# Sixteen gate products, four pool products and eight sums of squares: from fp32 matmuls to products of high and low parts

## The chip, the cores and the metric

The kernel runs on one core of a Trainium2 chip. Its time is the device time of one execution, in microseconds (us). A median is that of several executions; a profile is one further execution, recorded by the hardware profiler. The engines are TensorE (PE, with its weight loads as PEld), VectorE (DVE), ScalarE (ACT), GpSimd (POOL) and SyncE (SP), which here only issues DMAs.

## The reference

Two layers work on x of 512 tokens by 1024 channels, all in float32. A layer is a half-step SwiGLU feed-forward network (FFN), a token mixer, and a second FFN; an RMSNorm ends the whole. The mixer projects its normed input once (`proj = h @ w_in`) and splits the result among three branches. The three places that matter here are these:

```
# branch A, pooling: centred window means minus the token, then a map per group of 64 channels
mixed = einsum('bsgc,gcd->bsgd', mixed, pool_w)
# branch B, differential attention: RMSNorm of each head's output
o = o * rsqrt(mean(o * o, axis=-1) + SUBLN_EPS) * subln_g
# branch C, RG-LRU, in two directions: xf is a depthwise conv of lx over the tokens, width 4
r = sigmoid(einsum('bsgc,gcd->bsgd', xb, w_a) + b_a)
i = sigmoid(einsum('bsgc,gcd->bsgd', xb, w_x) + b_x)
a = exp(-8 * r * softplus(-lam)); u = sqrt(-expm1(2 * log a)) * (i * xf); h = scan(a, u)
```

Each branch is projected to 1024 channels, gated, summed, and projected once more.

## The kernel before

All activations stand channel by channel on the 128 partitions, with the 512 tokens along the free axis, so nearly every product is a 128x128 weight tile times a 128x512 tile. The large products are done in fp32r, a float32 form that PE takes in one pass and that holds fewer bits. To keep the accuracy each operand is split in two: `hilo(src)` copies the source into an fp32r tile on ACT (the high part) and puts a subtraction for DVE (source minus high: the low part) on the list `later`. `flush()` records what is on that list. `mm3` is then three matmuls into one PSUM bank: high by high, weight high by data low, weight low by data high. Weights are split in the same way, into `wh` (ACT) and `wl` (DVE). A few small products are left as plain fp32 matmuls: the LRU gates `r` and `i` (weights `bd`, data `xf`), the pool map (`bdp` by `pw`), and the attention's sums of squares `nrm` (a matrix of ones by `q`, the square of a head's output `o`).

All the instructions of an engine run in the order in which they are recorded, and the order is that of a list `units`. A unit is a stretch of PE work, mostly 24 matmuls on one weight block. After each unit comes a `gap`: here the list `later` is flushed, hooks run (`add_hook(n, fn)` puts `fn` into the gap of unit n), weights of later units are split, and side threads get a turn. The side threads are lists of steps: "lru" (conv, gates, scans), "pool" (window means, pool map), "sc" and "av" (scores and weighted values of the attention). A step runs in a gap if it lies at least as many gaps behind the step before it as its entry says (`apart`), and if a rough clock that the program keeps for ACT and DVE is not too far ahead of the one that it keeps for PE. That clock counts an fp32 matmul four times, so the change alters it a little.

The mixer begins with the two units of `lx` (named `ps<-z,wh` and `ps<-z,wl` in the trace). Ahead of them x is transposed (`zt`) and split into eight pairs of `z`; the first four are made in one gap, by four ACT instructions for the high parts and four DVE instructions for the low parts. Then `mixer_R` makes R, the norm factor of each token, and `lx` is scaled by it. The units of `v` follow, and between them run the steps of "lru": a conv for each of the two channel tiles (one ACT and three DVE instructions on a tile of `xf`), then four pairs of gates, one `r` and one `i` matmul each, and ACT and DVE work on them. Later come the units of q and k, gate logits and, at the end of the mixer, the units `y`, which project the branches; the last of them (`y<-at`) multiply the normed attention output `at`, which waits for `nrm` of the last head.

In the trace nearly every instruction has line L83, that of the helper that records them, so that they are told apart by the names of their tiles.

Of the kernel before, what the change touches and what calls it, by code (L numbers as in the profile page):

```python
# [107 lines left out]
def trunk_kernel(ctx, tc, xn, pm, fin, cst, bd, f1i, f1o, win, wbp, wba, wbl, wout, f2i, f2o, out):  # L108
# [29 lines left out]
    def f(t):  # L138
        return t.bitcast(F32)
# [8 lines left out]
    def hilo(src, name):  # L148

        hi, lo = pair(F32R, name)  # L150
        A.activation(out=hi, in_=src, func=AF.Copy)
        later.append(lambda: V.tensor_tensor(out=lo, in0=src, in1=f(hi), op=SUB))
        return hi, lo

    def mm3(acc, wh, wl, zh, zl, first, last):
        PE.matmul(acc, lhsT=wh, rhs=zh, start=first, stop=False)
        PE.matmul(acc, lhsT=wh, rhs=zl, start=False, stop=False)
        PE.matmul(acc, lhsT=wl, rhs=zh, start=False, stop=last)
# [5 lines left out]
    sp4 = cp_.tile([128, DEPTH * 4], F32, tag="sp4", name="sp4")  # L164
    nlam = cp_.tile([128, DEPTH], F32, tag="nlam", name="nlam")
    subg = cp_.tile([128, DEPTH], F32, tag="subg", name="subg")
    ident = cs[:, C_ID:C_ID + 128]
    ones = cs[:, C_ONE:C_ONE + 128]

# [16 lines left out]
    def add_hook(i, fn):  # L186
        hooks.setdefault(i, []).append(fn)
# [9 lines left out]
        V.scalar_tensor_tensor(out=r, in0=t, scalar=1.5, in1=y0, op0=ADD, op1=MUL)  # L197
        return r

    def inv_rms_start(acc, n, eps, col):  # L200

        ps = bank("nrm")
        PE.matmul(ps, lhsT=ones, rhs=acc, start=True, stop=True)
        y0, m = two("y0")
        A.t += 2.6
        A.activation(out=y0, in_=ps, func=AF.Abs_reciprocal_sqrt, scale=1.0 / n, bias=cs[:, C_EPS + col:C_EPS + col + 1])
        V.tensor_scalar(out=m, in0=ps, scalar1=1.0 / n, scalar2=eps, op0=MUL, op1=ADD)
        return y0, m
# [499 lines left out]
    def mixer(l, side, done, between):  # L708
# [20 lines left out]
        def conv(c):  # L729
            if c == 0:  # L730
                xf[:] = two("xf")
            t = xf[c]
            A.activation(out=t, in_=lx[c], func=AF.Identity, scale=pc(l, "cw", 2 * 2 + c), bias=pc(l, "cb", c))
            for j, (o0, o1, i0) in ((0, (2, S, 0)), (1, (1, S, 0)), (3, (0, S - 1, 1))):
                V.scalar_tensor_tensor(
                    out=t[:, o0:o1], in0=lx[c][:, i0:i0 + o1 - o0], scalar=pc(l, "cw", 2 * j + c), in1=t[:, o0:o1], op0=MUL, op1=ADD)
            lx[c] = None

        def lru_gate(d, c):
            e = d * 2 + c  # L740
            r, i = bank("r"), bank("i")
            PE.matmul(r, lhsT=g["bd"][:, e * 128:(e + 1) * 128], rhs=xf[c], start=True, stop=True)
            PE.matmul(i, lhsT=g["bd"][:, (4 + e) * 128:(5 + e) * 128], rhs=xf[c], start=True, stop=True)
            (th, ix), (a, t) = two("thr"), two("a")
            A.activation(out=th, in_=r, func=AF.Tanh, scale=0.5, bias=hab[:, l * 8 + e:l * 8 + e + 1])
            A.activation(out=ix, in_=i, func=AF.Tanh, scale=0.5, bias=hab[:, l * 8 + 4 + e:l * 8 + 5 + e])
            sc = sp4[:, l * 4 + e:l * 4 + e + 1]
            A.activation(out=a, in_=th, func=AF.Exp, scale=sc, bias=sc)
            A.activation(out=t, in_=th, func=AF.Tanh, scale=sc, bias=sc)
            A.activation(out=th, in_=a, func=AF.Square)  # L750
            lru[d, c] = (a, t, ix, th)
# [99 lines left out]
        def pool_win(c):  # L851
            P = pads.pop(c)
            W, o = big(name="padw"), slot(name="pw")
            tt = lambda out_, i0, i1: V.tensor_tensor(out=out_, in0=i0, in1=i1, op=ADD)
            if c == 0:
                tt(o[0:64], P[0:64, 15:527], P[0:64, 16:528])
                tt(W[64:128, 0:543], P[64:128, 0:543], P[64:128, 1:544])
                tt(o[64:128], W[64:128, 14:526], W[64:128, 16:528])
            else:
                tt(W[:, 0:543], P[:, 0:543], P[:, 1:544])  # L860
                tt(W[:, 0:541], W[:, 0:541], W[:, 2:543])
                tt(o[0:64], W[0:64, 12:524], W[0:64, 16:528])
                tt(W[64:128, 0:537], W[64:128, 0:537], W[64:128, 4:541])
                tt(o[64:128], W[64:128, 8:520], W[64:128, 16:528])
            e0 = C_EDGE + c * 16
            for t0, k in ((0, 0), (S - 8, 8)):
                V.tensor_tensor(out=o[:, t0:t0 + 8], in0=o[:, t0:t0 + 8], in1=cs[:, e0 + k:e0 + k + 8], op=MUL)
            V.scalar_tensor_tensor(out=o, in0=o, scalar=cs[:, C_INVW + c:C_INVW + c + 1], in1=P[:, 16:528], op0=MUL, op1=SUB)
            g["pw", c] = o

        def pool_mm(c):
            ps = bank("pool")
            PE.matmul(ps, lhsT=g["bdp"][:, c * 128:(c + 1) * 128], rhs=g.pop(("pw", c)), start=True, stop=True)
            hi, lo = pair(F32R, "ph")
            A.activation(out=hi, in_=ps, func=AF.Copy, scale=pc(l, "ps", c))
            V.scalar_tensor_tensor(out=lo, in0=ps, scalar=pc(l, "ps", c), in1=f(hi), op0=MUL, op1=SUB)
            g["pool", c] = (hi, lo)
# [148 lines left out]
        def subln_sq(h):  # L1026
            o, q = two("o")
            V.tensor_copy(out=o, in_=av.pop(h))
            A.activation(out=q, in_=o, func=AF.Square)
            g["o", h] = (o, q)  # L1030

        def subln(h):
            o, q = g.pop(("o", h))
# [99 lines left out]
        def load_bd():  # L1133
            g["bd"], g["bdp"] = big(name="bd"), slot(name="bdp")[:, 0:256]
            SP.dma_start(out=g["bd"], in_=bd[l][:, 0:1024])
            SP.dma_start(out=g["bdp"], in_=bd[l][:, 1024:1280])


        n0 = len(units)
        b = proj(OFF_LX)  # L1140
        for c in range(2):
            tile128(b, c, after_lx(c))
        add_hook(n0, load_bd)
        v_units()

        def qkheads(h0):
# [202 lines left out]

    def derived_steps():  # L1350
        def halves():
            for l in range(DEPTH):
                V.tensor_scalar(out=hmb[:, l * 24:l * 24 + 24], in0=pcs(l, "mb"), scalar1=0.5, scalar2=None, op0=MUL)
                V.tensor_scalar(out=hab[:, l * 8:l * 8 + 8], in0=pcs(l, "bab"), scalar1=0.5, scalar2=None, op0=MUL)
                V.tensor_scalar(out=subg[:, l:l + 1], in0=pcs(l, "sub"), scalar1=1.0 - LAM_INIT[l], scalar2=None, op0=MUL)


        n = DEPTH * 4
        lam = par[:, LAM0:LAM0 + n]
        w, q, s, p = small(n), small(n), small(n), small(n)  # L1360

        def start():
            A.activation(out=w, in_=lam, func=AF.Abs)
            A.activation(out=w, in_=w, func=AF.Exp, scale=-1.0)
            V.tensor_scalar(out=q, in0=w, scalar1=2.0, scalar2=None, op0=ADD)
            V.reciprocal(q, q)
            V.tensor_tensor(out=s, in0=w, in1=q, op=MUL)
            V.tensor_tensor(out=q, in0=s, in1=s, op=MUL)
            V.memset(p, 0.0)

        def series(ns):
            for k in ns:
                V.scalar_tensor_tensor(out=p, in0=p, scalar=1.0 / k, in1=q, op0=ADD, op1=MUL)

        def end():
            V.scalar_tensor_tensor(out=p, in0=p, scalar=1.0, in1=s, op0=ADD, op1=MUL)
            V.tensor_scalar(out=w, in0=lam, scalar1=-1.0, scalar2=0.0, op0=MUL, op1=MAX)
            V.scalar_tensor_tensor(out=w, in0=p, scalar=2.0, in1=w, op0=MUL, op1=ADD)
            V.tensor_scalar(out=sp4, in0=w, scalar1=-4.0, scalar2=None, op0=MUL)


        pr = small(2 * DEPTH)

        def lam_dot():
            for l in range(DEPTH):
                lp = pcs(l, "lp")
                V.tensor_tensor(out=pr[:, 2 * l:2 * l + 1], in0=lp[:, 0:1], in1=lp[:, 1:2], op=MUL)
                V.tensor_tensor(out=pr[:, 2 * l + 1:2 * l + 2], in0=lp[:, 2:3], in1=lp[:, 3:4], op=MUL)

        def lam_sum():  # L1390
            ps = bank("lam")
            PE.matmul(ps[:, 0:2 * DEPTH], lhsT=ones, rhs=pr, start=True, stop=True)
            e = small(2 * DEPTH)
            A.activation(out=e, in_=ps[:, 0:2 * DEPTH], func=AF.Exp)
            for l in range(DEPTH):
                V.tensor_tensor(out=nlam[:, l:l + 1], in0=e[:, 2 * l + 1:2 * l + 2], in1=e[:, 2 * l:2 * l + 1], op=SUB)
                V.tensor_scalar(out=nlam[:, l:l + 1], in0=nlam[:, l:l + 1], scalar1=-LAM_INIT[l], scalar2=None, op0=ADD)

        yield 0.5, halves, True
        yield 0.8, start, True  # L1400
        yield 0.8, lambda: series((19, 17, 15, 13, 11)), True
        yield 0.8, lambda: series((9, 7, 5, 3)), True
        yield 0.8, end, True
        yield 0.4, lam_dot, True
        yield 0.4, lam_sum, True
# [214 lines left out]
```

## Time and profile before

| what | value |
|---|---|
| median of 3 runs | 2115.81 us (2114.51 to 2118.64) |
| the profiled execution | 2117.74 us, of which its span is 2115.9 us |
| PE busy | 2072.8 us, 98% of the span |
| DVE busy | 1658.6 us, 78% |
| ACT busy | 1191.2 us, 56% |
| mean granted clock of TensorE | 0.997 of full speed |

PE is busy nearly all the time, so that the span is the sum of its matmuls and of some waits: it exceeds PE's busy time by 43.1 us. The busy time of a matmul counts from its start to its end, and matmuls overlap: what a matmul adds to the span is the distance from its start to that of the next, not its length.

### The profile page before, as it was taken

The numbers are of one execution on the slowest core, as the hardware profiler recorded it, in microseconds if no ns is written. First come the engines' busy times: TensorE is split into PE (matmuls) and PEld (weight loads), VectorE is DVE, ScalarE is ACT, GpSimd is POOL, SyncE is SP. The second block draws the span as 40 slices with busy tenths as digits, with TensorE's granted clock in tenths as the row PEclk, the third lists the DMA queues.
The fourth block names the chain that finished last, engine by engine and source line by source line (L and its number), as shares of the span: only waits on it lengthen the run. The fifth ranks groups of instructions, "written<-read, shape, count | busy, mean of one in ns | idle before, by whom it ended". The sixth has DMA issues, their size and how long they took to land.

```text
span 2115.9 us, 26228 instructions
## 1 busy us (share of the span) xinstructions
PE 2072.8 (98%) x9646; PEld 1734.1 (82%) x9646; DVE 1658.6 (78%) x2362; ACT 1191.2 (56%) x1766; POOL 343.7 (16%) x292
## 2 busy tenths in 40 slices
PE   8999999999999999999999999999999999999998
PEld 6988888788787889888879887887887877988786
DVE  6788898597677588779977878986967766788797
ACT  7555566645663565556755555665456536555564
POOL 1312230000000022213213222300000001322230
PEclk9999999999999999999999999999999999999999
DMA  9987997022226379889959879940221364887994
GB/s 252 180 184 159 210 193 216 1 79 90 70 80 189 80 148 193 162 203 196 228 104 205 172 157 239 183 154 20 84 82 54 117 180 79 163 192 164 205 179 102
DMA packets 194096, 314.61 MB, mean 149 GB/s; under 512 B 10544, under 2 KB 86832, under 8 KB 193968
## 3 DMA queue, kind: packets, MB, share of 16 engines
q0 software_dynamic: 76288, 138.43, 39.5%
q1 hardware_dynamic: 117392, 174.30, 24.8%
q8 instruction: 75, 1.23, 0.2%
q14 instruction: 53, 0.43, 0.1%
q10 hardware_dynamic: 288, 0.21, 0.0%
HBM read 310.80 MB, written 2.10 MB: 148 GB/s over the span
## 4 chain that ended last, share of the span: by engine, by line
PE 80%; DVE 9%; ACT 4%; DMA 4%; issue 2%; POOL 1%; DVEq 0%; SPq 0%; POOLq 0%; ACTq 0%
PE P L83 26%; PE Q L83 19%; PE ps L83 18%; PE o L83 4%; PE y L83 4%; DVE wl L83 4%; DMA raw<-in_f1i_dram 2%; PE v L83 2%; PE ht L83 2%; PE sc L83 1%; PE av L83 1%; ACT wh L83 1%; ACT zh L83 1%; DVE c L83 1%; DVE x L83 1%
## 5 line engine op out<-in xcount | busy, mean ns | idle before, releaser
L83 DVE TENSOR_TENSOR wl<-raw,wh 128x1024 fp32r<-128x1024 f32 (+2 forms) x696 | 705.7, 1038 | 163.4 <-ACT wh L83 153.7
L83 ACT ACTIVATE wh<-raw 128x1024 fp32r<-128x1024 f32 (+2 forms) x695 | 606.9, 906 | 208.2 <-DMA raw<-in_f2i_dram 53.0
L83 PE MATMUL ps<-z,wh 128*128 128x512 f32 x1216 | 380.1, 393 | 0.2
L372 POOL DMA_DIRECT2D raw<-in_f2i_dram x96 | 116.0, 1240 | 1114.4 <-DVE mg L83 353.2
L83 PE MATMUL P<-wl,zh 128*128 128x512 f32 (+1 forms) x768 | 287.3, 374 | 7.2 <-DVE wl L83 7.1
L83 PE MATMUL P<-wh,zh 128*128 128x512 f32 (+1 forms) x768 | 288.7, 376 | 4.7 <-ACT wh L83 3.1
L83 PE MATMUL P<-wh,zl 128*128 128x512 f32 (+1 forms) x768 | 286.5, 373 | 0.5 <-DVE zl L83 0.5
L83 PEld LDWEIGHTS ps<-z,wh 128*128 128x128 f32 x1216 | 227.1, 188 | 51.1 <-issue 3.4
L83 PE MATMUL ps<-z,wl 128*128 128x512 f32 x608 | 237.0, 390 | 0.0
L83 PE MATMUL Q<-wl,zh 128*128 128x512 f32 (+1 forms) x576 | 214.6, 373 | 6.1 <-DVE wl L83 6.1
L83 PE MATMUL Q<-wh,zh 128*128 128x512 f32 (+1 forms) x576 | 216.7, 376 | 2.1 <-ACT zh L83 1.9
L83 PE MATMUL Q<-wh,zl 128*128 128x512 f32 (+1 forms) x576 | 214.2, 372 | 1.0 <-DVE zl L83 1.0
L372 POOL DMA_DIRECT2D raw<-in_f1i_dram x96 | 116.1, 1236 | 366.9 <-DVE wl L83 274.2
L83 PEld LDWEIGHTS P<-wl,zh 128*128 128x128 f32 x768 | 145.1, 189 | 30.5 <-DVE wl L83 10.4
L83 PEld LDWEIGHTS P<-wh,zh 128*128 128x128 f32 x768 | 144.8, 189 | 25.7 <-ACT wh L83 3.5
L83 PEld LDWEIGHTS P<-wh,zl 128*128 128x128 f32 x768 | 145.0, 189 | 21.3 <-DVE zl L83 1.0
L83 PE MATMUL P<-wl,ah 128*128 128x512 f32 x352 | 138.1, 392 | 2.4 <-DVE wl L83 2.3
L83 PE MATMUL P<-wh,ah 128*128 128x512 f32 x352 | 137.5, 391 | 0.0
L83 PE MATMUL P<-wh,al 128*128 128x512 f32 x352 | 137.2, 390 | 0.0
L83 PEld LDWEIGHTS ps<-z,wl 128*128 128x128 f32 x608 | 114.1, 188 | 23.7
L83 PEld LDWEIGHTS Q<-wl,zh 128*128 128x128 f32 x576 | 108.2, 188 | 23.1 <-DVE wl L83 9.2
L83 PEld LDWEIGHTS Q<-wh,zh 128*128 128x128 f32 x576 | 108.2, 188 | 17.3 <-ACT zh L83 2.7
(192 smaller groups left out, 3414.4 us busy)
## 6 DMA issues: line engine op xcount, KB each, us to landing
raw<-in_win_dram SPq DMA_DIRECT2D x84, 512.0 KB, 4.7
raw<-in_f1i_dram POOLq DMA_DIRECT2D x64, 512.0 KB, 6.9
raw<-in_f2i_dram POOLq DMA_DIRECT2D x64, 512.0 KB, 6.9
raw<-in_f2i_dram SPq DMA_DIRECT2D x52, 512.0 KB, 5.5
raw<-in_f1i_dram SPq DMA_DIRECT2D x50, 512.0 KB, 6.2
raw<-in_f1o_dram POOLq DMA_DIRECT2D x40, 512.0 KB, 7.9
raw<-in_f2o_dram POOLq DMA_DIRECT2D x40, 512.0 KB, 8.3
raw<-in_f1o_dram SPq DMA_DIRECT2D x30, 512.0 KB, 7.5
```

What stands on the lines that cost most here:

```text
L83: return fn(*args, **kw)
L372: return lambda raw: GP.dma_start(out=raw[:, 0:n * w].rearrange("p (k f) -> p k f", f=w), in_=src, accum_op=ADD)
```

## The change

The three kinds of fp32 products become fp32r products of split parts. A gate (`lru_gate`) and a pool map (`pool_mm`) are now `mm3`, three matmuls; a sum of squares is two, a matrix of ones (`oner`, copied once at the start) by the high and by the low part of `q`. So each operand has to be split: `xf` into `xs` at the end of its conv, the pooled tile into `pw`, the squares into `qs`, and the gate and pool weights into `bh`, `bl` and a pair `bdp`, in a new function `split_bd`. That runs as a hook in the gap ahead of the first `lx` unit, and the hook that loads those weights is moved eight gaps earlier. A low part that `hilo` puts on the list is recorded at the next flush.

```diff
+    oner = cp_.tile([128, 128], F32R, tag="oner", name="oner")
...
-    def inv_rms_start(acc, n, eps, col):
+    def inv_rms_start(parts, n, eps, col):
         ps = bank("nrm")
-        PE.matmul(ps, lhsT=ones, rhs=acc, start=True, stop=True)
+        for i, part in enumerate(parts):
+            PE.matmul(ps, lhsT=oner, rhs=part, start=i == 0, stop=i == 1)
...
             lx[c] = None
+            g["xf", c] = hilo(t, "xs")
...
-            PE.matmul(r, lhsT=g["bd"][:, e * 128:(e + 1) * 128], rhs=xf[c], start=True, stop=True)
-            PE.matmul(i, lhsT=g["bd"][:, (4 + e) * 128:(5 + e) * 128], rhs=xf[c], start=True, stop=True)
+            bh, bl = g["bd"]
+            for ps, o in ((r, e * 128), (i, (4 + e) * 128)):
+                mm3(ps, bh[:, o:o + 128], bl[:, o:o + 128], *g["xf", c], True, True)
...
-            g["pw", c] = o
+            g["pw", c] = hilo(o, "pw")
...
-            PE.matmul(ps, lhsT=g["bdp"][:, c * 128:(c + 1) * 128], rhs=g.pop(("pw", c)), start=True, stop=True)
+            bh, bl = (a[:, c * 128:(c + 1) * 128] for a in g["bdp"])
+            mm3(ps, bh, bl, *g.pop(("pw", c)), True, True)
...
-            g["o", h] = (o, q)
+            g["o", h] = (o, hilo(q, "qs"))
...
+        def split_bd():
+            both = pair(F32R, "bdp")
+            for name, (hi, lo) in (("bd", (big(F32R, "bh"), big(F32R, "bl"))), ("bdp", [a[:, 0:256] for a in both])):
+                src = g[name]
+                A.activation(out=hi, in_=src, func=AF.Copy)
+                later.append(lambda lo=lo, src=src, hi=hi: V.tensor_tensor(out=lo, in0=src, in1=f(hi), op=SUB))
+                g[name] = (hi, lo)
...
-        add_hook(n0, load_bd)
+        add_hook(n0 - 8, load_bd)
+        add_hook(n0 - 1, split_bd)
```

Where the instructions go is shown at two places of the first layer's mixer; the second layer has the same rows. First ACT, from the norm of x (`m`) at the mixer's start to the table load ahead of the first gate's tanh. Before:

```order
186 L83 ACTIVATE m<-m 128x2
187 L83 ACTIVATE wh<-raw 128x512 x2
188 L83 ACTIVATE z<-zt,par 128x512 x4
189 L83 ACTIVATE R<-rb 128x512
190 L83 ACTIVATE wh<-raw 128x512 x2
191 L83 ACTIVATE xf<-lx,par 128x512 x2
192 L83 ACT_TABLE_LOAD
```

And of the change:

```order
186 L83 ACTIVATE m<-m 128x2
187 L83 ACTIVATE bh<-bd 128x1024
188 L83 ACTIVATE bdp<-bdp 128x256
189 L83 ACTIVATE wh<-raw 128x512 x2
190 L83 ACTIVATE z<-zt,par 128x512 x4
191 L83 ACTIVATE R<-rb 128x512
192 L83 ACTIVATE wh<-raw 128x512 x2
193 L83 ACTIVATE xf<-lx,par 128x512
194 L83 ACTIVATE xs<-xf 128x512
195 L83 ACTIVATE xf<-lx,par 128x512
196 L83 ACTIVATE xs<-xf 128x512
197 L83 ACT_TABLE_LOAD
```

The high parts `bh` and `bdp` stand ahead of the two weight splits and the high parts of `z`, and the high part `xs` of each conv stands between that conv and the next. On DVE, at the mixer's start, before:

```order
322 L83 TENSOR_SCALAR m<-m 128x2
323 L83 TENSOR_TENSOR m<-m 128x2
324 L83 TENSOR_TENSOR wl<-raw,wh 128x512 x2
325 L83 SCALAR_TENSOR_TENSOR z<-zt,par,z 128x512 x4
326 L83 TENSOR_SCALAR rb<-cst,m 128x128 x4
```

And of the change:

```order
323 L83 TENSOR_SCALAR m<-m 128x2
324 L83 TENSOR_TENSOR m<-m 128x2
325 L83 TENSOR_TENSOR bl<-bd,bh 128x1024
326 L83 TENSOR_TENSOR bdp<-bdp 128x256
327 L83 TENSOR_TENSOR wl<-raw,wh 128x512 x2
328 L83 SCALAR_TENSOR_TENSOR z<-zt,par,z 128x512 x4
329 L83 TENSOR_SCALAR rb<-cst,m 128x128 x4
```

The low parts `bl` and `bdp` now stand ahead of the weights' low parts and the four of `z`. Further on DVE, from `lx` to the work on the first gate, where the rows of 510 and 511 tokens are the conv steps, three for each tile. Before:

```order
327 L83 TENSOR_TENSOR lx<-ps,R 128x512 x2
328 L83 SCALAR_TENSOR_TENSOR xf<-lx,par,xf 128x510
329 L83 SCALAR_TENSOR_TENSOR xf<-lx,par,xf 128x511 x2
330 L83 SCALAR_TENSOR_TENSOR xf<-lx,par,xf 128x510
331 L83 SCALAR_TENSOR_TENSOR xf<-lx,par,xf 128x511 x2
332 L83 TENSOR_TENSOR wl<-raw,wh 128x512 x2
```

And of the change:

```order
330 L83 TENSOR_TENSOR lx<-ps,R 128x512 x2
331 L83 SCALAR_TENSOR_TENSOR xf<-lx,par,xf 128x510
332 L83 SCALAR_TENSOR_TENSOR xf<-lx,par,xf 128x511 x2
333 L83 SCALAR_TENSOR_TENSOR xf<-lx,par,xf 128x510
334 L83 SCALAR_TENSOR_TENSOR xf<-lx,par,xf 128x511 x2
335 L83 TENSOR_TENSOR xs<-xf,xs 128x512 x2
336 L83 TENSOR_TENSOR wl<-raw,wh 128x512 x2
```

Both low parts of `xf` stand behind the six conv steps, in one row. PE's own order there, before:

```order
1541 L83 MATMUL v<-wh,z 128x512
1542 L83 MATMUL r<-xf,bd 128x512
1543 L83 MATMUL i<-xf,bd 128x512
1544 L83 MATMUL v<-wh,z 128x512
1545 L83 MATMUL v<-wl,z 128x512
```

And of the change:

```order
1541 L83 MATMUL v<-wh,z 128x512
1542 L83 MATMUL r<-xs,bh 128x512 x2
1543 L83 MATMUL r<-xs,bl 128x512
1544 L83 MATMUL i<-xs,bh 128x512 x2
1545 L83 MATMUL i<-xs,bl 128x512
1546 L83 MATMUL v<-wh,z 128x512
1547 L83 MATMUL v<-wl,z 128x512
```

The gate still stands at the same place among the matmuls of `v`; its second matmul is the first to read a low part.

## Rows read from the trace of the kernel before

**Rows 1.** The page: busy time by engine; chain that ended last, by engine.
```profile
...
PE 2072.8 (98%) x9646; PEld 1734.1 (82%) x9646; DVE 1658.6 (78%) x2362; ACT 1191.2 (56%) x1766; POOL 343.7 (16%) x292
...
PE 80%; DVE 9%; ACT 4%; DMA 4%; issue 2%; POOL 1%; DVEq 0%; SPq 0%; POOLq 0%; ACTq 0%
```

**Rows 2.** Windows: us, busy us (count) by engine, PEclk, DMA share, GB/s.
```profile
...
340.00:700.00 360.00, 358.13 (x1596) 290.70 (x1595) 266.83 (x471) 192.49 (x328) 2.41 (x2) 1.00 0.30 92
1385.00:1745.00 360.00, 358.12 (x1596) 290.67 (x1595) 266.96 (x471) 192.51 (x328) 2.41 (x2) 1.00 0.30 92
1080.70:1083.70 3.00, 3.00 (x8) 2.34 (x7) 1.91 (x2) 1.06 (x2) 1.20 (x1) 0.50 0.04 6
```

**Rows 3.** Timeline of PE, first gate: start, us, engine, instruction, count.
```profile
...
376.61 1.02 PE L83 MATMUL r<-xf,bd 128*128 128x512 f32 x2
377.47 1.02 PE L83 MATMUL i<-xf,bd 128*128 128x512 f32 x2
```

**Rows 4.** Timeline of PE around one matmul of squares.
```profile
...
533.08 0.39 PE L83 MATMUL ps<-z,wl 128*128 128x512 f32 x1
533.31 1.02 PE L83 MATMUL nrm<-o,cst 128*128 128x512 f32 x2
...
534.63 0.40 PE L83 MATMUL ps<-z,wl 128*128 128x512 f32 x1
```

**Rows 5.** Timeline of ACT and DVE ahead of the first gate.
```profile
...
371.83 1.14 ACT L83 ACTIVATE wh<-raw 128x512 fp32r<-128x512 f32 x2
...
372.87 1.51 ACT L83 ACTIVATE xf<-lx,par 128x512 f32<-128x512 f32 x2
...
373.71 4.55 DVE L83 SCALAR_TENSOR_TENSOR xf<-lx,par,xf 128x510 f32<-128x510 f32 x6 [0.45 <-ACT xf L83]
...
378.18 1.28 DVE L83 TENSOR_TENSOR wl<-raw,wh 128x512 fp32r<-128x512 f32 x2
```

**Rows 6.** Timeline, start of the first layer's mixer: PE, ACT and DVE.
```profile
...
362.27 1.14 ACT L83 ACTIVATE wh<-raw 128x512 fp32r<-128x512 f32 x2
...
363.09 1.91 PE L83 MATMUL zt<-cst,x 128*128 128x128 f32 x16
363.13 1.29 DVE L83 TENSOR_TENSOR wl<-raw,wh 128x512 fp32r<-128x512 f32 x2
363.79 2.43 ACT L83 ACTIVATE z<-zt,par 128x512 fp32r<-128x512 f32 x4 [0.38 <-PE zt L83]
364.51 2.73 DVE L83 SCALAR_TENSOR_TENSOR z<-zt,par,z 128x512 fp32r<-128x512 f32 x4
...
364.75 1.06 PE L83 MATMUL ps<-z,wh 128*128 128x512 f32 x2
```

**Rows 7.** Groups by form: busy time, mean ns; idle before, its end.
```profile
...
L83 ACT ACTIVATE wh<-raw 128x1024 fp32r<-128x1024 f32 x403 | 413.7, 1052 | 141.8 <-DMA raw<-in_f2i_dram 53.0 <-DMA raw<-in_f1i_dram 48.8 <-DVE wl L83 24.6
...
L83 DVE TENSOR_TENSOR wl<-raw,wh 128x1024 fp32r<-128x1024 f32 x404 | 485.7, 1219 | 116.4 <-ACT wh L83 115.6 <-issue 0.3
```

**Rows 8.** Timeline of PE in three stretches of FFNs; in brackets idle before.
```profile
...
41.32 0.49 PE L83 MATMUL P<-wh,zh 128*128 128x512 f32 x1 [3.11 <-ACT wh L83]
...
43.22 0.63 PE L83 MATMUL P<-wh,zh 128*128 128x512 f32 x1
...
45.78 0.63 PE L83 MATMUL P<-wh,zh 128*128 128x512 f32 x1
...
1068.12 0.33 PE L83 MATMUL zt<-cst,x 128*128 128x128 f32 x1 [2.88 <-DVE x L83]
...
1080.39 0.54 PE L83 MATMUL P<-wh,zl 128*128 128x512 f32 x1 [0.53 <-DVE zl L83]
```

**Rows 9.** Timeline of PE, last unit of the first layer's attention branch.
```profile
...
656.46 0.61 PE L83 MATMUL y<-at,wh 128*128 128x512 f32 x2
...
660.54 1.02 PE L83 MATMUL nrm<-o,cst 128*128 128x512 f32 x2
...
666.57 0.49 PE L83 MATMUL y<-at,wh 128*128 128x512 f32 x1 [0.88 <-ACT at L83]
```

More of the change, by code (lines that the diff above doesn't have):

```diff
@@ L741, in lru_gate @@
             r, i = bank("r"), bank("i")
-            PE.matmul(r, lhsT=g["bd"][:, e * 128:(e + 1) * 128], rhs=xf[c], start=True, stop=True)
-            PE.matmul(i, lhsT=g["bd"][:, (4 + e) * 128:(5 + e) * 128], rhs=xf[c], start=True, stop=True)
+            bh, bl = g["bd"]
+            for ps, o in ((r, e * 128), (i, (4 + e) * 128)):
+                mm3(ps, bh[:, o:o + 128], bl[:, o:o + 128], *g["xf", c], True, True)
+            if d == 1:
+                del g["xf", c]
             (th, ix), (a, t) = two("thr"), two("a")
@@ L1351, in halves @@
         def halves():
+            V.tensor_copy(out=oner, in_=ones)
             for l in range(DEPTH):
```

## The prediction

> **What bounds the kernel now.** The page comes first. PE is busy for 2072.8 of 2115.9 us, and it holds 80% of the chain that ended last [rows 1]. The change touches the two mixers, so the next view is the windows: in 360 us of either mixer PE is busy for 358.1, DVE for 267 and ACT for 192.5, and the granted clock is 1.00, the level of 2.4 GHz [rows 2]. The two rows are alike, and I cost the first layer and double it. The reader is to see that inside the mixer a matmul taken off PE's stream is a gain at full price, that ACT and DVE have a quarter or more of their time free on average, and that this average is no help at a place where PE is waiting for one split: there the queue of that engine decides. So I read the timeline around each place at which the new order has new rows.
>
> **What PE gains.** An fp32 matmul stands in the trace as two records; from the start of `r` to that of `i` it is 377.47 − 376.61 = 0.86 us [rows 3]. For the fp32r stream, one record of `wl` to the next with one fp32 matmul of squares among three fp32r ones takes 534.63 − 533.08 = 1.55 us [rows 4]. If that fp32 matmul costs 0.87, the three cost 0.68, or 0.227 each, and the same holds of every undisturbed stretch. With that:
> - gates: 2 layers x 4 pairs x 2 = 16 fp32 matmuls, each now three of fp32r: 16 x (0.863 − 0.68) = 2.9;
> - pool maps: 4 x (0.88 − 0.68) = 0.8, the same shape as the squares and priced by their row;
> - squares: 8, each now two: 8 x (0.87 − 0.454) = 3.3.
>
> Together 7.1 us. That is all that the change can give.
>
> **What the new splits cost where PE waits for nothing.** Per layer ACT gets two `xs`, two `pw` and four `qs` of 128x512, `bh` of 128x1024 and a `bdp` of 128x256, DVE as many low parts. In a row, a 128x512 one takes 0.57 on ACT and 0.64 on DVE (half of the pairs of 1.14 and 1.28) [rows 5]; for one by itself, which hands its result on, I take a tenth more as an estimate, 0.63 and 0.69. With 1.05 and 1.22 for 128x1024 [rows 7] that is 6 to 7 us on each, out of 167 and 93 us free [rows 2]. The splits of `pw` and `qs` stand one gap, some 24 matmuls or 5.4 us, ahead of their product; what hides them is that stretch of PE work, and if it were gone a split would cost 0.63 + 0.69 = 1.3 each. For the last head's squares the cover is thinner: its operands are wanted after the first y matmuls of that unit, and between 656.46 and 660.54 PE has 4.08 us of them [rows 9], more than the copy, the square, its high and its low part need (0.69 + 0.63 + 0.63 + 0.69 = 2.6, and some 0.2 to 0.6 to hand over). I take 0 and keep 0 to 1.3 per layer for the range; the wait of 0.88 for `at` [rows 9] I leave as it is. The load of `bd` moves eight gaps up on SP's queue, ahead of weight loads, and these weights' splits on ACT wait for DMAs of the two FFNs alone by the row [rows 7]: 0. The copy of ones is one small instruction at the start: 0.
>
> **First loss: the first gate.** Here the order of rows decides. On DVE the six conv steps took 4.55 us from 373.71, 0.76 apart [rows 5], so that those of the first tile ended at 375.98, and PE started `r` at 376.61 without a wait [rows 3]. Now the chain is: high part `xs` on ACT from 376.02 to 376.65; then ACT's conv instruction of the second tile, 0.75 [rows 5], to 377.40; then three steps on DVE, 2.28, to 379.67; and only then, in DVE's order, the low part of the first tile, 0.69 with the start of the next overlapping: ready at 380.3. The first matmul of `r` needs only the high part and goes at about 376.7. The second reads the low part. Without a stall it would start at 376.84. So PE stands for 380.3 − 376.84 = 3.5 us, with the other matmuls of `r`, all of `i` and the next unit of `v` behind it; on ACT the table load and the tanh of the gates are late with it, but they follow PE. Behind the low parts on DVE stand two `wl`, which before began at 378.18 [rows 5], and now end at about 382.3; they belong to the next unit, which PE reaches 5 us after the gate. Nothing is given back later, since PE is the bound: 2 x 3.5 = 7.0. Bounds: 0, if DVE did the low part before the conv of the second tile, which its order excludes; and 4.3 per layer, if the second conv instruction is delayed by another 0.8.
>
> **Second loss: the start of the mixer.** Here PE already waits on ACT and DVE: two matmuls of `ps` take 1.06 us together where the rule is 0.62, the second being held by the first low part of `z`, which starts on DVE at 364.51 [rows 6]. In front of it, DVE did two `wl` from 363.13; ACT had done their high parts from 362.27 and those of `z` from 363.79 [rows 6]. Now `bh` (1.05 [rows 7]) and `bdp` (0.35 to 0.4, from the two larger forms by size) go first on ACT, `bl` (1.14 to 1.22) and `bdp` (0.35) on DVE. ACT begins `bh` at 362.27 and ends at 363.3; DVE begins `bl` at 363.36 and comes to the weights' low parts at 364.84, and to `z` 1.29 later, at 366.1 in place of 364.5. That is 1.5 us, with 0.1 for rounding left out. Behind it stand the other three low parts, 0.68 apart as PE's own steps are, `rb` and the norm factor, so nothing catches up before the four are done. The end of `zt` at 365.0 [rows 6] leaves PE no other work. 2 x 1.5 = 3.1 with the hundredths. Bounds: 1.0 per layer if the `wl` pair, which waits for the same ACT, closes up, and 1.7 if every instruction takes its full length.
>
> **The clock.** In the trace a stop of PE costs more than its length in some places. After an idle of 3.11 us (41.32) seven matmuls from 43.22 to 45.78 stood 2.56 / 6 = 0.43 apart [rows 8], twice the 0.227 of elsewhere; with one more at the edge, eight at 0.20 are 1.6 us. After the idle of 0.53 at 1080.39 [rows 8] the granted clock was 0.50 for 3 us, the level of 1.2 GHz [rows 2], though that stop was short. A stop of 2.88 at 1068.12 [rows 8] was followed by none that I found. The stall at the gate leaves PE idle for about 3.3 to 3.4 us, more than the longest of these stops. The Trainium skill, in TensorE: Matmul & The Clock Gate, section Why this matters for your kernels, advises against idle gaps of PE between bursts of matmuls, since the clock drops to half after one; by it both gate stalls would pay the 1.6 as well. The trace agrees at 41.32 and does not settle it for the new places. I price a fall at each gate stall, 2 x 1.6 = 3.2 (two in three for each), and none at the start of the mixer, where PE stops for 1.3 in one piece (one in three).
>
> **The sum.** −7.1 + 7.0 + 3.1 + 3.2 = +6.2 us. From the profiled execution (2117.74, of which 2115.9 span) that is 2123.9. The profiled execution lies 1.9 above the median of the runs, so that on the median, 2115.81, I expect 2122.0.
>
> **The rivals.**
> - *The stalls come, the clock holds.* Speaks for it: 2.88 us of idle left the clock at full speed [rows 8]. −7.1 + 10.1 = +3.0, or 2118.8.
> - *One of the two stalls is absorbed.* If the 3.1 at the mixer's start is hidden by instructions that ran earlier than I read, and the clock holds, the sum is −7.1 + 7.0 = −0.1; if the gate's is half as long, −7.1 + 3.5 + 3.1 = −0.5. Either is 2115.5 or so. For it: DVE is busy for three quarters of the mixer only [rows 2]; against it: an engine's rows can't overtake each other, and both places have the new rows in front.
> - *The splits keep up, and the gain stands:* −7.1, or 2108.7. The one mechanism is at the first gate: its low part would have to be ready when PE arrives. It decides at the point where DVE does the low part of the first tile before the conv steps of the second, which needs the steps to be 2.3 us earlier (or the gate 3.5 us later). Against it: DVE's rows stand in one order, and `r` came 0.6 us after the first tile's steps, with no room for two passes of 0.63 and 0.69. With both mechanisms half as large as read and no clock loss, the sum is −2, on the same side as no change.
> - *The change does not do what it says:* fp32r matmuls at the price of fp32 would make the sum worse by some 20 us; the stream of `v` and `ps` in the same form speaks against it, and I give it nothing.
>
> **How the numbers follow.** A measurement of this kernel can tell about 0.2%, 4.2 us, from no change: faster is below 2111.6, slower above 2120.0. Both stalls with one to four falls of the clock: 0.60, between 2120.4 and 2125.4, likeliest at 2122.0. Stalls without a fall: 0.22, 2118.8. One stall absorbed: 0.09, 2115.5. The splits keep up: 0.09, 2108.7 to 2111. So slower 0.60, the same 0.31, faster 0.09. The range leaves out the last case and the upper bounds of a few (both gates 0.8 longer, the last head's squares 1.3): 2116.0 to 2127.0; the likeliest case's own is 2120 to 2126.
>
> **What would show it.** Right: in the profile after, PE waits on `r` for DVE `xs` twice, about 3.4 each, and on `ps` for DVE `z` twice, about 1.7 each with what was there; the records of `r`, `i`, `pool` and `nrm` stand 0.23 apart; the granted clock of the 4 us behind each gate stall is near 0.5; the waits on `y` for `at` are as before. Wrong: no wait on `r`, or one under 2 us, would mean that the low part of `xs` came earlier; a clock of 1.00 behind the gates takes 1.6 off for each; a new wait on `nrm`, `pool` or `y` would mean that a split which I hid is on the path.

## The result and the profile after

| kernel | median | range | runs |
|---|---|---|---|
| before | 2115.16 us | 2113.76 to 2118.64 | 4 |
| change | 2133.04 us | 2131.19 to 2134.16 | 4 |

The ratio is 1.0084, with a 95% interval of 1.0072 to 1.0096: slower by 17.9 us, where 6.2 was forecast and 2127 was the top of the range. The profiled execution of the change took 2132.38 us.

The first lines are the page's, busy time and the chain by engine, to be set against [rows 1].

```profile
...
PE 2074.7 (97%) x9666; PEld 1743.7 (82%) x9666; DVE 1672.9 (79%) x2383; ACT 1202.4 (56%) x1786; POOL 343.7 (16%) x292
...
PE 70%; DVE 18%; ACT 8%; issue 3%; DMA 1%; POOL 0%; DVEq 0%; ACTq 0%; POOLq 0%
```

PE is busy for 2074.7 us, about as long as before, though it has less to do: the span grew by 14.3 and its idle time by 12.4. The chain runs through DVE and ACT for 26%, not 13%. The mixers show the same in the windows that answer to [rows 2]; the other rows are stretches behind stops, at the first gate and for `wl`, of the first and of the second layer:

```profile
...
340.00:700.00 360.00, 349.31 (x1563) 286.15 (x1562) 271.56 (x480) 197.79 (x338) 2.41 (x2) 0.99 0.28 90
1385.00:1745.00 360.00, 349.29 (x1564) 286.18 (x1563) 271.75 (x478) 199.22 (x339) 2.41 (x2) 0.99 0.29 92
381.80:385.20 3.40, 3.27 (x8) 2.63 (x9) 1.97 (x5) 2.90 (x5) 0.00 (x0) 0.50 0.00 0
613.90:617.30 3.40, 3.40 (x10) 2.63 (x9) 1.44 (x3) 2.41 (x5) 0.00 (x0) 0.50 0.00 0
1433.20:1439.80 6.60, 5.51 (x13) 4.40 (x14) 3.80 (x7) 5.54 (x8) 0.00 (x0) 0.50 0.00 0
1666.00:1670.00 4.00, 4.00 (x18) 3.29 (x19) 1.69 (x4) 2.73 (x5) 0.00 (x0) 1.00 0.00 0
```

PE is busy for 349.3 of 360 us, 8.8 less than before in either mixer. At the first gate the granted clock fell to 0.50, the level of 1.2 GHz, in both layers, and PE worked at that level for 3.3 us in the first (381.8) and for 5.5 us in the second (1433.2). It fell once more in the first layer (613.9), behind a stop of 2.0 us for `wl` that ended at 612.4; behind the same stop of the second layer (1666.0) it stayed at 1.00. What PE waits for stands in the list of its waits (us in total, times, longest), of which these are new or changed:

```profile
...
PE r L83 <- DVE xs L83: 6.3, 2, 3.2
PE ps L83 <- DVE wl L83: 4.6, 4, 2.0
...
PE ps L83 <- ACT wh L83: 2.4, 2, 1.2
PE ps L83 <- DVE z L83: 2.1, 2, 1.0
...
PE av L83 <- DVE gt L83: 1.6, 2, 0.8
...
PE ps L83 <- DVE k L83: 1.0, 2, 0.5
PE ps L83 <- ACT z L83: 0.6, 2, 0.3
```

The waits on `r` (3.2 each) and on `z` (1.0, with 0.3 on ACT's `z`) are those of the prediction. Those on `wl`, `wh`, `gt` and `k`, 9.6 us over the two layers, are not in it. Where the first layer stands in the end is told by the first wait of `y` for `at`:

```profile
...
676.47 0.49 PE L83 MATMUL y<-at,wh 128*128 128x512 f32 x1 [0.93 <-ACT at L83]
```

That row stood at 666.57 [rows 9]: the first layer's mixer lost 9.9 us to this point. The second layer has the same waits at the same places. Over the whole span 14.3 were lost in this profile, less than twice 9.9, since the FFNs behind the mixers happened to run some 5 us faster in it than in the profile of before. The FFN stretch between the two mixers varies by 4 us over the profiles of this document (671.4 to 675.6), while the two mixers of one kernel agree within 0.1 us where their clock is the same. So a mixer is the better ruler. It is measured below from PE's first `ps` matmul in it (357.64 in the kernel before) to the `y` that waits for `at` (666.57): 308.9 us.

### The profile page after: what moved, and what is told of

It reads as the page before. It is cut to its first block, busy times and chain, and to the rows that moved or that the text cites. A ratio compares the mean times of both kernels' runs of the same rounds, so it can differ in the third digit from the quotient of the medians.

```text
span 2130.2 us, 26303 instructions
## 1 busy us (share of the span) xinstructions
PE 2074.7 (97%) x9666; PEld 1743.7 (82%) x9666; DVE 1672.9 (79%) x2383; ACT 1202.4 (56%) x1786; POOL 343.7 (16%) x292
## 4 chain that ended last, share of the span: by engine, by line
PE 70%; DVE 18%; ACT 8%; issue 3%; DMA 1%; POOL 0%; DVEq 0%; ACTq 0%; POOLq 0%
PE P L83 28%; PE Q L83 18%; PE ps L83 10%; DVE wl L83 6%; PE o L83 4%; PE y L83 3%; ACT wh L83 2%; PE ht L83 2%; PE v L83 2%; DMA raw<-in_f2i_dram 1%; DVE x L83 1%; DVE c L83 1%; PE sc L83 1%; DVE kl L83 1%; ACT e L83 1%
## 5 line engine op out<-in xcount | busy, mean ns | idle before, releaser
L83 PEld LDWEIGHTS Q<-wh,zl 128*128 128x128 f32 x576 | 108.1, 188 | 17.0 <-DVE zl L83 1.9
```

Of the source, the lines that this page charges most:

```text
L83: return fn(*args, **kw)
```

## The experiments

Twelve kernels ran, in three groups on three chips. Each was timed against the kernel before on its own chip, where that had medians of 2112.58, 2112.79 and 2113.62 us, so that kernels of different groups are compared by their distance to before. "Side threads held" in an edit means that a table of gaps, read from one of the two kernels, decides in which gap a step of a side thread runs, in place of the rough clock.

### Do the side threads cost it? same_places and places_alone

The change also makes the steps of the "pool", "sc" and "av" threads run one gap later, since the rough clock counts the new work. One kernel is the change with the gaps of before, the other the kernel before with the gaps of the change.

```diff
+GAPS = {'av': [[149, 150, 151, ...], ...], 'pool': [[141, 142], [452, 453]], ...}
...
-                    if not force and (t[3] + apart > self.gap or max(V.t, A.t) + cost > PE.t + AHEAD):
+                    if not force and self.gap < t[5]:
```

> The change, but each step of the side threads runs in the gap in which it ran before the change. Theory A: of the 19.3 us that the two mixers lost, some 9 come from the side threads, which ran a gap later and piled up on DVE and ACT (per layer: 2.0 on a late wl and 1.7 of clock behind it, 0.5 and 0.8 on k and gt). Then 2133 becomes about 2124, and those waits are gone, while the gate's 3.2, the one on z and the 1.5 behind the pool tiles stay. Theory B: the new splits of pw and qs themselves make these waits, wherever the steps stand; then it stays at 2131 to 2135.

> The kernel before, with nothing split, but each step of the side threads in the gap in which the change puts it. Theory A: 2115 becomes about 2124, with the waits on wl, k and gt of the change at the same places, and a fall of the clock. Theory B: no difference, 2113 to 2117.

same_places: 2131.88 against 2112.58, ratio 1.0088 (1.0074 to 1.0102), +19.3 us. places_alone: 2111.83 against 2112.58, ratio 0.9996 (0.9987 to 1.0005). Both are what theory B said, and theory A fell on both sides: the later gaps cost nothing by themselves, and with the old ones the change loses as much as before, at other waits (`pool` for `pw` in place of `ps` for `wh`; `sc` and `wT` in place of `ps` for `wl`). So it is the splits.

### Which of the three? gates_alone, pool_alone, squares_alone

Each leaves two of the three products as fp32 matmuls, side threads held at their gaps of before.

```diff
-            g["o", h] = (o, hilo(q, "qs"))
+            g["o", h] = (o, q)
```

> Only the sixteen gate products as fp32r (xs, bh, bl; no bdp, pw, qs), the side threads in their gaps of before. The prediction's own terms: -2.9 from PE, +7.0 from the stall at the first gate, +2.4 at the mixer's start (bl without bdp), +3.2 from the clock: +9.7 over before, which is 2122.3 against 2112.6. Rival: the gates pay more elsewhere too, as the squares did; then above 2125.

> Only the four pool products as fp32r (bdp, pw), the side threads in their gaps of before. Theory C (rows held up in order): the high part of pw waits on ACT for DVE's window sums of 5 us, its low part on DVE for ACT, and the next unit's weight splits stand behind both. Then PE waits some 1.3 per layer at the product and 1.2 at the next unit, and bdp costs some 0.4 at the mixer's start: +3 to +6 less 0.8, that is 2115 to 2118. Rival (hidden by the unit of PE work between, as predicted): -0.8, 2111.8.

> Only the eight sums of squares as two fp32r matmuls, with the side threads where they were before. By the row for the fp32 matmul (0.87) against two of 0.227 it gains 8 x 0.42 = 3.3: 2111.8. If the qs rows hold up what stands behind them on DVE and ACT, the gain is 0 to 2: 2113 to 2115.

gates_alone: 2123.03 against 2112.79, 1.0048 (1.0035 to 1.0060), +10.2 where the prediction's own terms said +9.7. pool_alone: 2117.40 against 2112.79, 1.0019 (1.0010 to 1.0028), +4.6. squares_alone: 2115.58 against 2112.58, 1.0014 (1.0005 to 1.0023), +3.0. Together 17.8, beside the 19.3 of all three: the parts add up within their intervals. The mixers of the profiles say the same with less noise: per layer the gates add 6.0 us, the pool maps 1.7, the squares 1.2, together 8.9, and all three with the side threads held (same_places) 9.5. The gates come to the forecast in their sum. The pool maps, whose terms in the prediction make −0.1 (0.8 gained, 0.7 for `bdp` at the mixer's start), and the squares, at −3.3, are where the forecast went wrong.

The pool maps first, in the timeline of pool_alone at the second tile:

```profile
...
454.55 0.75 DVE L91 SCALAR_TENSOR_TENSOR pw<-pw,cst,pad 128x512 f32<-128x512 f32 x1
...
455.33 0.63 ACT L91 ACTIVATE pw<-pw 128x512 fp32r<-128x512 f32 x1 [5.13 <-DVE pw L91]
...
456.00 0.69 DVE L91 TENSOR_TENSOR pw<-pw 128x512 fp32r<-128x512 f32 x1 [0.70 <-ACT pw L91]
...
456.02 0.49 PE L91 MATMUL pool<-pw,bdp 128*128 128x512 f32 x1 [1.07 <-ACT pw L91]
...
456.74 0.73 PE L91 MATMUL pool<-pw,bdp 128*128 128x512 f32 x2 [0.23 <-DVE pw L91]
```

The window sums fill DVE up to 455.3, and PE reaches the product at 455.0; the high part can only be copied then, and the low part a copy later. PE waits 1.07 and 0.23. The kernel before had these rows at the same place, with its DVE over the 30 us around it:

```profile
...
454.45 0.75 DVE L83 SCALAR_TENSOR_TENSOR pw<-pw,cst,pad 128x512 f32<-128x512 f32 x1
...
455.31 1.07 PE L83 MATMUL pool<-pw,bdp 128*128 128x512 f32 x2
...
440.00:470.00 30.00, 30.00 (x130) 24.01 (x129) 29.25 (x54) 9.14 (x15) 0.00 (x0) 1.00 0.31 97
```

Its sums ended at 455.2, 0.1 us before the product, and DVE was busy for 29.25 of the 30 us (its figure is the third of the engines', behind PE and PEld). So no room for a split was there, though the sums are recorded a gap ahead of the product. In the change itself the product stands a gap later, and the price is paid by what is queued behind the copy on ACT. Its timeline there:

```profile
...
460.18 0.75 DVE L83 SCALAR_TENSOR_TENSOR pw<-pw,cst,pad 128x512 f32<-128x512 f32 x1
460.96 0.63 ACT L83 ACTIVATE pw<-pw 128x512 fp32r<-128x512 f32 x1 [5.12 <-DVE pw L83]
461.50 1.14 ACT L83 ACTIVATE wh<-raw 128x512 fp32r<-128x512 f32 x2
...
462.17 0.73 PE L83 MATMUL ps<-z,wh 128*128 128x512 f32 x2 [1.18 <-ACT wh L83]
```

ACT stands 5.12 us for DVE's `pw`, and the two weight splits `wh` of the next unit are behind the copy in its order, so PE waits 1.18 for `wh`. Before, with no copy in front, no weight split waited for the window sums.

For the squares, the timeline of squares_alone at the second head of the first layer:

```profile
...
574.57 0.68 DVE L91 COPY o<-av 128x512 f32<-128x512 f32 x1
...
575.29 0.63 ACT L91 ACTIVATE o<-o 128x512 f32<-128x512 f32 x1
...
575.96 0.63 ACT L91 ACTIVATE qs<-o 128x512 fp32r<-128x512 f32 x1
...
576.62 0.69 DVE L91 TENSOR_TENSOR qs<-o,qs 128x512 fp32r<-128x512 f32 x1 [1.36 <-ACT qs L91]
...
577.23 1.22 DVE L91 TENSOR_TENSOR wl<-raw,wh 128x1024 fp32r<-128x1024 f32 x1
...
578.37 0.68 DVE L91 TENSOR_TENSOR gt<-ps,R 128x512 f32<-128x512 f32 x1
...
584.11 0.50 PE L91 MATMUL sc<-kh,qa 128*128 128x512 f32 x1 [0.33 <-DVE gt L91]
```

After its copy of `o` DVE stands 1.36 us, until ACT has squared it and copied the high part; then comes the low part, and only then `wl` and the eviction `gt`. In the profile of before these two stood 2.1 earlier:

```profile
...
575.12 1.22 DVE L83 TENSOR_TENSOR wl<-raw,wh 128x1024 fp32r<-128x1024 f32 x1
576.25 0.68 DVE L83 TENSOR_TENSOR gt<-ps,R 128x512 f32<-128x512 f32 x1
```

The last row of squares_alone is a matmul of the scores, one unit later, that waits for the next `gt`, which is as late.

### Is it the order, or the work? squares_low_late and squares_high_only

The first puts the low part of `qs` behind `wl` of its gap. The second leaves the low part out: ACT writes the square directly as fp32r and one matmul sums it, so that no work is added to ACT or DVE.

```diff
             g["o", h] = (o, hilo(q, "qs"))
+            tail.append(later.pop())
...
         for fn in lows:
             fn()
+        while tail:
+            tail.pop(0)()
```

> The squares alone, but with the low part of qs recorded behind the low parts of the weights of its gap. Theory C: what made the squares alone slower by 3.0 is that DVE stood for 1.36 us per head for ACT's square and high part, with wl and the eviction gt behind it; with wl in front, the wait is covered and 0.65 of work per head is left: 2109 to 2111, below before by 2 to 3. Rival D: it is the added work on DVE and ACT, not the order; then it stays near 2115.

> The squares with the high part alone: ACT writes the square as fp32r and one matmul sums it; the low part is left out, and so nothing is added on ACT or DVE. PE saves 8 x (0.87 - 0.23) = 5.1. If the stretch around the sums of squares waits only for PE, all of it reaches the end: 2107.7. If the stretch of k and kl waits for DVE and ACT, the first head's saving is swallowed there, 0.64 per layer: 2109. If the waits on kh and gt that the squares alone had come without the added rows too, 2111 or more.

squares_low_late: 2113.70 against 2112.79, 1.0004 (0.9995 to 1.0012). DVE's stop shrinks from 1.36 to 0.23:

```profile
...
574.83 0.69 DVE L91 COPY o<-av 128x512 f32<-128x512 f32 x1
...
575.44 1.22 DVE L91 TENSOR_TENSOR wl<-raw,wh 128x1024 fp32r<-128x1024 f32 x1
...
576.88 0.69 DVE L91 TENSOR_TENSOR qs<-o,qs 128x512 fp32r<-128x512 f32 x1 [0.23 <-ACT qs L91]
...
577.49 0.68 DVE L91 TENSOR_TENSOR gt<-ps,R 128x512 f32<-128x512 f32 x1
```

Some 2 us of the loss are gone with the order (a mixer is 0.1 us longer than before, in squares_alone 1.2), but there is no gain. Per layer the trace has four steps of −0.4 at the four sums, and takes them back: 0.4 at the waits of the scores for `kh` and `kl`, behind the first of them, and 1.3 at 584 to 592, where a PSUM bank that `gt` reads comes free late. squares_high_only: 2109.93 against 2113.62, 0.9982 (0.9973 to 0.9990), −3.7 of 5.1, as the second of its three cases has it; the interval, 2.1 to 5.7, does not by itself exclude the first. By the trace, without added rows the second of these two losses is gone (no wait there), and the first stays: the wait of the scores for `kh` is 0.41. So the added work counts in that stretch too, not the order alone; both theories hold a part. And there a saving on PE ends in part in a longer wait, though no work was added.

### The two stalls of the prediction: gates_low_early and gates_bd_hidden

```diff
+            if c == 1:
+                g["xf", 0] = hilo(xf[0], "xs")
+                low = later.pop()
             for j, (o0, o1, i0) in ((0, (2, S, 0)), (1, (1, S, 0)), (3, (0, S - 1, 1))):
                 V.scalar_tensor_tensor(...)
+                if low:
+                    low()
+                    low = None
```

> The gates alone, with the low part of the first xf recorded behind the first of the second conv's three steps. The prediction's two terms at the first gate: the stall of 3.2 to 3.5 per layer and the clock's 1.6 behind it. Both gone but for some 0.5 per layer: 2123.0 becomes 2113.5, with a granted clock of 1.00 behind the gate. Rival: the clock fell for another reason (the start of the mixer); then the fall stays and it is 2116.5.

2113.29 against 2113.62, 0.9996 (0.9987 to 1.0005), −0.3 where gates_alone had +10.2: 10.5 are gone, where 9.5 were expected. The wait on `r` is 0.23 in place of 3.17. The wait of 1.02 on `z` at the mixer's start is still there, so it is not what took the clock down. The windows of gates_alone and then of this kernel behind the gate:

```profile
...
382.20:386.00 3.80, 3.80 (x9) 3.03 (x10) 2.44 (x4) 3.30 (x5) 0.00 (x0) 0.50 0.00 0
```

```profile
...
378.00:382.00 4.00, 4.00 (x18) 3.34 (x19) 3.17 (x5) 2.57 (x4) 0.00 (x0) 1.00 0.02 4
```

The stall is what took the clock down: without it, it stays at 1.00. All eight stalls on `r` in the four profiles that have them (the change, same_places, gates_alone, gates_bd_hidden) had a fall behind them, and no kernel without the stall had one there.

In the other, `split_bd` runs inside `mixer_R`, with `bl` recorded behind `rb`.

> The gates alone, with the split of bd moved to where DVE and ACT stand idle: bh behind the four high parts of z, bl behind rb, in the 3.9 us for which DVE waited for R. If the loss at the mixer's start is the order (bl ahead of z), it is gone, 1.2 per layer: 2123.0 becomes 2120.6. If it is the extra work, it comes back at R or lx: 2122 to 2123.

2121.76 against 2113.62, 1.0034 (1.0022 to 1.0045), +8.1 in place of gates_alone's +10.2: 2.1 less, where 2.4 were expected. The two intervals overlap, so the trace decides: the wait of 1.02 on `z` that gates_alone has at the mixer's start is not there, and PE waits for neither R nor `lx`. The row of gates_alone:

```profile
...
367.04 0.50 PE L91 MATMUL ps<-z,wh 128*128 128x512 f32 x1 [1.02 <-DVE z L91]
```

### Mended: all_mended, all_mended_2 and gates_mended

The first two keep all three products and move the splits: `split_bd` into an earlier gap, the low part of the first `xf` forward, `pw` and `qs` as told in the expectations.

> The change with four things mended: the side threads in their gaps of before, the low part of the first xf ahead of two of the second conv's steps, split_bd three gaps earlier, and the pool tiles split a gap later than made (their product a gap later too). If the lost time is these four places, what is left is the gain of 7.1 less about 0.6 per layer at the gate: 2109. If the splits cost something by themselves wherever they stand, 2112 to 2118.

> All three products as fp32r with the splits put where they hold up least: xs of the first tile ahead of two of the second conv's steps and the second behind wl; bd split five gaps earlier, its low parts behind wl; the high part of pw behind wh and its low part behind wl, its product a gap later; the low part of qs behind wl; side threads in their gaps of before. Theory C: 7.1 less 0.8 per layer at the gate and some 0.6 per layer at the pool: 2108 to 2110. Rival D: the added 7 us of DVE work per layer cost a part whatever the order: 2113 to 2118.

all_mended: 2121.25 against 2112.58, 1.0040 (1.0028 to 1.0053), above both cases of its expectation. all_mended_2: 2117.91 against 2112.79, 1.0025 (1.0014 to 1.0035), at the top of what its rival D said. Both lie 9 us or more below the change by their distance to before, and neither beats the kernel before. In both the split of `bd` stands in the last units of the FFN, and there it makes DVE 1.5 us late with `x`, on which the mixer's start hangs: the waits at the first `ps` are still 0.51 (ACT) and 0.60 (DVE). A gap that looks early is not idle for that.

These waits are only 1.1 us per layer, while the mixers miss the gain of 3.6 per layer by 7.8 (all_mended) and 5.9 (all_mended_2). Much of the rest stands at the pool tiles and at the scores: per layer all_mended waits 1.1 for `pw` at a pool product and 1.0 for `kh`. In all_mended_2 the wait for `pw` is gone, but the low part of the first pool tile (0.7) now stands ahead of the second tile's window sums, and `wl` behind them is late:

```profile
...
450.66 0.69 DVE L91 TENSOR_TENSOR pw<-pw 128x512 fp32r<-128x512 f32 x1
...
456.65 1.28 DVE L91 TENSOR_TENSOR wl<-raw,wh 128x512 fp32r<-128x512 f32 x2
...
457.39 0.50 PE L91 MATMUL ps<-z,wl 128*128 128x512 f32 x1 [0.75 <-DVE wl L91]
```

So at the pool tiles, where DVE has no time to spare, the added work costs in every order that was tried. No run moves the pool split alone.

gates_mended does the gates alone, in this way:

```diff
-        add_hook(n0 - 1, split_bd)
+        add_hook(n0 - 1, lambda: st.update(split=split_bd))
...
     # in mixer_R, behind rb on DVE and ahead of R on ACT
+        st.pop("split")()
+        flush()
...
-            for ps, o in ((r, e * 128), (i, (4 + e) * 128)):
-                mm3(ps, bh[:, o:o + 128], bl[:, o:o + 128], *g["xf", c], True, True)
+            for w, x_, first, last in ((bh, xh, True, False), (bl, xh, False, False), (bh, xl, False, True)):
+                for ps, o in ((r, e * 128), (i, (4 + e) * 128)):
+                    PE.matmul(ps, lhsT=w[:, o:o + 128], rhs=x_, start=first, stop=last)
```

> The gates alone with both mended, and the low parts used last: for each pair of gates the four products with the high part of xf come first, those with its low part last. The gain of 2.9 should be left whole: 2112.8 becomes 2110, or 2111 if some of it is lost at waits later in the mixer.

2109.70 against 2113.62, ratio 0.9982 (0.9973 to 0.9990): faster than the kernel before, by 3.9 us (2.1 to 5.7) where 2.9 was the gain by rows. The mixers of its profile are 1.3 us shorter each, 2.6 together; the rest of the 3.9 is not told apart from the noise of the FFNs. Its timeline at the two places:

```profile
...
366.84 0.86 DVE L91 TENSOR_SCALAR rb<-cst,m 128x128 f32<-128x128 f32 x4
...
367.62 1.21 DVE L91 TENSOR_TENSOR bl<-bd,bh 128x1024 fp32r<-128x1024 f32 x1
...
371.65 1.29 DVE L91 TENSOR_TENSOR lx<-ps,R 128x512 f32<-128x512 f32 x2 [2.81 <-ACT R L91]
...
376.47 0.69 DVE L91 TENSOR_TENSOR xs<-xf,xs 128x512 fp32r<-128x512 f32 x1
...
376.49 0.50 PE L91 MATMUL r<-xs,bh 128*128 128x512 f32 x1
...
376.83 0.40 PE L91 MATMUL i<-xs,bh 128*128 128x512 f32 x1
...
377.53 0.39 PE L91 MATMUL r<-xs,bh 128*128 128x512 f32 x1
```

`bl` fits in the time for which DVE waits for R (2.81 us are left of the 3.95 before, in the row below), and the four matmuls with the high part cover the low one: no wait stands on these rows of `r` and `i`.

```profile
...
371.97 1.29 DVE L83 TENSOR_TENSOR lx<-ps,R 128x512 f32<-128x512 f32 x2 [3.95 <-ACT R L83]
```

## Why the prediction was wrong

- **What PE gains** (7.1): right in size. Each sum of squares shows a step of 0.4 in every kernel that splits it, and gates_mended kept 2.6 us in its mixers, beside 2.9 by rows. (The pool map is put at 0.88, where the squares' row gives 0.87; the sum is the same.)
- **First gate** (3.5 per layer): right; 3.16 in the wait. Recording the low part earlier removed it.
- **Start of the mixer** (1.5 per layer): right; the waits are 1.05 for DVE's and 0.29 for ACT's `z`, and PE's matmuls behind them stand 1.5 later. gates_bd_hidden removed it.
- **Clock** (1.6 per gate stall): right that both stalls bring a fall, and shown to hang on the stall. By the rule of the Trainium skill's TensorE: Matmul & The Clock Gate, section Why this matters for your kernels, both gate stalls had to pay, and in the trace both do. The size was right in the first layer alone: PE worked at 0.50 for 3.3 us there, which is 1.6 lost, but for 5.5 us in the second layer, which is 2.8; in the profile of gates_alone it is 5.7 and 5.5 us. The term was priced from one fall, at 41.32, and the falls are not all of one length. The change has a further fall that was not forecast, in the first layer behind the stop of 2.0 for `wl`, 1.7 us. So in its profile the clock took 6.1 us, where 3.2 was priced. That gates_alone came to +10.2 beside +9.7 is thus no proof of this price: its profiled execution was the slowest of its five (2125.49), and the mean clocks, 0.993 in it and 0.995 to 0.996 in the others, speak for less time at half speed in those. And the stop at 1080.39, which the prediction took as one of 0.53, comes 1.3 us after another of 1.26.
- **Splits where PE waits for nothing** (0, kept at 0 to 1.3 per layer): this is the step that failed. The pool maps cost +4.6 in place of −0.1 and the squares +3.0 in place of −3.3, 11.0 of the 11.7 us by which the change missed its forecast (17.9 less 6.2). The step compared a split's own length with the PE work in its gap, and looked for its cost at the split's own product. The sign of being wrong that it gave, a new wait on `nrm`, `pool` or `y`, did not come in the change: the waits are those of other units' matmuls, on `wl`, `wh`, `gt` and `k`. It did not ask what is queued behind the split on ACT and DVE while it waits for its input: behind `pw` on ACT the next unit's `wh`, for 5.1 us of window sums; behind `qs` on DVE `wl` and an eviction, for 1.36 us of ACT. It had asked just that at the gate. At the second pool tile the gap of 5.4 us was no cover either: the trace of before has the end of the sums 0.1 us ahead of the product, on a DVE that is busy for 29.25 of 30 us, where the average of the mixer leaves a quarter free. In the stretch of the scores DVE is as free as on average (busy for 35.15 of the 47 us from 545 to 592), and there the order of the rows and their waits made the loss together with the added work.
- **The last head**, for which 0 to 1.3 was kept, was right at 0: `y` waits 0.93 for `at`, beside 0.88.
- The later gaps of the side threads, which the prediction left uncosted, cost nothing by themselves: −0.7 (places_alone), within the interval.
- **The rivals**: that the splits keep up was false for all three, but true of the gates once their low part stood ahead of the second conv's steps, as that rival's turning point said.

Not settled: how much of the squares' loss in the stretch of the scores is ACT's added row and how much DVE's; how much of the pool maps' loss is order and how much work; why one fall of the clock is longer than another; and the 1.5 us by which the whole is more than its parts, which is within the intervals.

## What to carry to other kernels

PE work between a split and its product does not make the split free: the engine that does it takes its instructions in order, so the price is also what stands behind the split for as long as it waits for its own input. So record a split behind the work that others wait for, or where its engine already stands idle, and use its result last. And judge slack in the very stretch, not over the stage: here DVE was free for a quarter of the mixer and for none of the pool tiles.

## What the runs showed of the hardware

In the profiled execution of squares_high_only the clock fell without a long stop: behind waits of 0.41, 0.26 and 0.38 us between 545.1 and 547.8 it was granted at 0.53 over 3.6 us, where the kernel before, with 0.25 and 0.38 at that place, kept it at 1.00. The windows of the one and of the other:

```profile
...
545.00:548.40 3.40, 2.30 (x8) 1.15 (x8) 2.63 (x4) 3.33 (x7) 0.00 (x0) 0.99 0.00 0
548.40:552.00 3.60, 3.60 (x14) 3.07 (x13) 3.50 (x6) 0.94 (x3) 0.00 (x0) 0.53 0.00 0
```

```profile
...
548.40:552.00 3.60, 3.60 (x21) 3.13 (x20) 3.19 (x6) 0.93 (x3) 0.00 (x0) 1.00 0.00 0
```

3.6 us at 0.53 are 1.7 us of work lost, and the second layer has the same at 0.55. So a saving on PE that ends in a wait can cost more than the wait. Whether the other executions of this kernel had these falls is not known; their mean clock was 0.995 to 0.997, beside 0.995 in this one.

A wait of a given length does not always bring a fall. In all_mended the scores of the first layer wait 1.00, 0.26 and 0.38 us, and so do those of the second; the windows behind the one and the other are these:

```profile
...
551.40:554.70 3.30, 3.30 (x13) 2.82 (x12) 3.21 (x6) 0.63 (x3) 0.00 (x0) 0.50 0.00 0
1597.00:1600.60 3.60, 3.47 (x19) 3.02 (x20) 2.79 (x6) 1.34 (x3) 0.00 (x0) 1.00 0.00 0
```

The same holds of the change's two stops of 2.0 us for `wl`, of which one had a fall behind it. Only the stalls of 3.2 us on `r` had one in all eight cases. So a fall behind a shorter wait is a risk to be priced with a chance, not a fixed term.
